# A two-layer hybrid encoder step: the eight PSUM banks of the first layer shared out anew

## The chip, the cores and the metric

The kernel runs on one core of a Trainium2 chip. A core has five engines, each with its own queue of instructions that it takes strictly in order: TensorE (PE in the profile; its weight loads are listed apart as PEld), VectorE (DVE), ScalarE (ACT), GpSimd (POOL) and SyncE (SP), which here mainly issues DMAs. TensorE writes its results into PSUM, 128 partitions wide, which this kernel uses as eight banks of 512 float32 columns. The other engines read PSUM and work on SBUF. Engines wait for each other through semaphores.

The metric is the device time of one execution in microseconds (us), lower is better.

## The reference

The kernel computes one inference step of two layers. Only the first layer's token mixer matters here: chunk-band attention with 16 heads of 64 channels, 2048 prompt rows, a band of 512 earlier rows, a learned bias by relative distance, and a gate path z from the same projection.

```python
def a_project(h, w_in, g_q, g_k):
    q, k, v, z = jnp.split(h @ w_in, 4, axis=-1)
    q = rms_norm(q.reshape(B, L, A_HEADS, A_HEAD_DIM), g_q)
    k = rms_norm(k.reshape(B, L, A_HEADS, A_HEAD_DIM), g_k)
    ...
def one_chunk(args):                      # 64 query rows against 512 + 64 key rows
    ...
    return attend(qi, kb, vb, rel_bias(table, qpos, kpos),
                  chunk_mask(qpos, kpos, A_BAND_CHUNKS), scale)
def attend(q, k, v, bias, mask, scale):
    s = jnp.einsum('bqhd,bkhd->bhqk', q, k).astype(jnp.float32) * scale
    s = jnp.where(mask[None, None], s + bias[None], NEG_INF)
    p = jax.nn.softmax(s, axis=-1).astype(v.dtype)
    return jnp.einsum('bhqk,bkhd->bqhd', p, v)
...
y = (o * jax.nn.silu(z)) @ w_out
```

Before it, each layer computes shift, scale and gate from the conditioning vector (`silu(c) @ W_ada + b_ada`), and beside the prompt a second group of 32 "sample" rows goes through the same mixer with a cache. The second layer is latent attention and keeps its own sharing of PSUM.

## The kernel before

**Numbers as pairs.** Operands of the matmuls are split into a high and a low half, so one product is three matmuls (helper `mm3`, lines 189 to 191). A projection chain over 1024 channels is 24 matmuls (8 x 3) into one bank.

**Steps.** The first layer's prompt attention is a list of 32 steps: two halves of the sequence, in each of them 8 pairs of heads (`g`), and for each pair two blocks of 512 rows (`blk`). I call the two steps of one head pair a cycle. In a step stand side by side, written as Python generators whose pieces a plan places at fractions of the step:

- `scores` and `values` of this step, for two heads and up to eight key tiles each. `scores` takes a bank of the kind `st` (lines 629, 630), VectorE adds bias or masks (633 to 637), ScalarE takes the exponential twice (643 into P, 644 into Ph), VectorE makes the low half Pl (645), GpSimd sums (647). Two tiles later `values` adds Ph and Pl times v (656, 657) into the bank of the head's output, kind `av`, which is taken once per head.
- `evac`: when a head is done, ScalarE copies one half of that bank (666) and VectorE adds the other half (667, the bank's last reader).
- `finish` of the step before: ScalarE casts a sum (675), the head pair's sums go through TensorE (680, 681, kind `mx`), VectorE takes reciprocals (687) and multiplies the gate z (688) and the output ob by it (689).
- `project` for the next step: four chains of 24 matmuls of 128x384, each into a bank of the kind `mm`. ScalarE copies each chain's bank to SBUF (481) and squares it (484).
- `project_z` for the next step: one chain of 24 matmuls of 128x512, kind `mm`, copied by ScalarE (513) into one of two SBUF tiles named z. The copy for one step needs the tile that line 689 of an earlier `finish` has read.
- `prep` for the next step: transposes (561) and row maxima of the scores (591 to 608), kind `mx`. Its matmuls need QG, which a DMA on SP's queue brings (its issue is line 104, a helper).

In steps 21 to 31 pieces of the second layer's conditioning (`ada_piece`) stand among these, in the last two steps the sample rows' attention (`sample_a`).

**PSUM.** The eight banks are fixed tiles. `psum_pool` gives each kind a list of them, and `bank(tag)` hands them out in turn; a tag without a list of its own takes from the list `mx`. In the rows the banks of `mm` are bank_66 and bank_70, of `st` bank_74 and bank_78, of `mx` bank_82, bank_86 and bank_90, of `av` bank_94. Later stages call `psum_pool` anew with their own numbers.

**Order.** The code's order is a wish: a scheduler (the Tile framework) sets the final order of each engine's queue when the kernel is built, and it knows which bank a tile lies in. TensorE's queue is one line: a matmul that waits for its bank holds up everything behind it.

Of the kernel before, what the change touches and what calls it, by code (L numbers as in the profile page):

```python
# [99 lines left out]
def trunk(ctx: ExitStack, tc: tile.TileContext, I, O, stop=99):  # L100
# [14 lines left out]
    def psum_pool(**bufs):  # L115
        i = 0
        psum.clear()
        for tag, n in bufs.items():
            psum[tag] = list(range(i, i + n))
            i += n  # L120

    psum_pool(mm=2, st=2, mx=3, av=1)

    S.preload_act_table_set("natural_log_exp_and_others")

# [67 lines left out]
    def bank(tag):  # L193
        order = psum[tag if tag in psum else "mx"]
        order.append(order.pop(0))
        return banks[order[-1]]
# [66 lines left out]
        gnorm.append(gn)  # L263

    def ada_part(i, pair, row, gc, sc, gn, adab, modr):
        acc = [bank("mm") for _ in range(2)]
        for k in range(KT):
            w = row()
            dma(w, I["ada_w"][i, 128 * k:128 * k + 128, 1024 * pair:1024 * pair + 1024])
            for n in range(2):  # L270
                T.matmul(acc[n][0:2, :], cT[:, k, :], w[:, 512 * n:512 * n + 512],
                         start=(k == 0), stop=(k == KT - 1))
        for n in range(2):
            mr = modr[:, 512 * n:512 * n + 512]
            V.tensor_tensor(mr, acc[n][0:2, :], adab[:, 512 * n:512 * n + 512], ALU.add)
            ada_use(i, pair, n, mr)
# [17 lines left out]
    def ada_piece(i, pair, n, a, ws, mr):  # L294

        c0 = 1024 * pair + 512 * n
        if a == 0:
            dma(mr, bass.AP(I["ada_b"].tensor, I["ada_b"].offset + 3 * i * D + c0, [[0, 2], [1, 512]]))
        for k in range(4):
            dma(ws[k], I["ada_w"][i, 512 * a + 128 * k:512 * a + 128 * k + 128, c0:c0 + 512])  # L300
        yield
        acc = bank("mm")[0:2, :]
        for k in range(4):
            T.matmul(acc, cT[:, 4 * a + k, :], ws[k], start=(k == 0), stop=(k == 3))
        V.tensor_tensor(mr, acc, mr, ALU.add)
        if a == 1:
            ada_use(i, pair, n, mr)
# [217 lines left out]
            split_z(s["next_g"], 1)  # L525

    def sample_rows(w, n, sec, g):
        p = bank("mm")[:, 0:n]
        for k in range(KT):
            for a in range(2):  # L530
                T.matmul(p[0:64, :], hsT[:, k, :], w(k, a), start=(k == 0 and a == 0), stop=(k == KT - 1 and a == 1))
        zt = at1([128, 4, 128], "hs").rearrange("p j t -> p (j t)")[0:NS, 0:n]
        S.copy(zt, p[32:64, :])
        V.tensor_tensor(zt, p[0:32, :], zt, ALU.add)
        if sec == 3:
            dma(zs_d[3, :, 128 * g:128 * g + 128], zt)
            return
        for h in range(2):
            c0 = 128 * g + 64 * h
            dma(zs_d[0:3, :, c0:c0 + 64].rearrange("s t d -> t s d"),  # L540
                zt[:, 192 * h:192 * h + 192].rearrange("t (s d) -> t s d", s=3))
# [293 lines left out]
    def sample_a(sp):  # L835
# [55 lines left out]
        for quad in range(4):  # L891
# [8 lines left out]
            if quad < 3:  # L900
                load_k(quad + 1)
            yield
            s0, s1 = bank("mm"), bank("mm")
            for p, ks in ((s0, [(kp[:, 0, :], kp[:, 1, :]) for kp in kps]),
                          (s1[:, 0:32], [(kn[:, quad, p2, 0:32], kn[:, quad, p2, 32:64]) for p2 in range(2)])):
                for p2 in range(2):
# [13 lines left out]
            S.copy(vn[:, 0, :], VR[0:32, qc])  # L920
            V.tensor_tensor(vn[:, 1, :], VR[0:32, qc], f32(vn[:, 0, :]), ALU.subtract)
            yield
            o = bank("mm")
            vals = [(vh[:, t, :], twin(nc, vraw[quad])[:, t, :]) for t in range(4)]
            pv_blocks(o[:, 0:256], PT, vals + [(vn[:, 0, :], vn[:, 1, :])], 544)
            diag_out(o, r, VR[zr, :], quad)
# [799 lines left out]
    for i in range(len(items) + LAG + 20):  # L1726
# [12 lines left out]
        if i >= LAG and fifo:  # L1739
            u, t, p = fifo.pop(0)  # L1740
            values(u, t, p)
            if t == u["order"][-1]:
                evac(u)
                later.append((i + DEN, denom, u))
                if u["blk"] % 2 and u["hd"] % 2:
                    n, u0 = INV if u["hd"] < 15 else (7, 9, 10, 10, 11), units[u["i"] - 1]
# [3 lines left out]
        while later and later[0][0] <= i:  # L1750
            _, f, u = later.pop(0)
            f(u)
        if i >= 100 and i % 25 == 0 and wload:
            k, n = wload.pop(0)
# [144 lines left out]
    def row(name):  # L1899
        return et([NS, D], name)  # L1900
# [62 lines left out]
```

## Time and profile before

| | |
|---|---|
| three timed runs | 3886.15, 3889.08 (median), 3892.15 us |
| the profiled execution's own time | 3874.33 us |
| its span, first to last instruction | 3872.2 us |
| mean granted TensorE clock | 0.956 |
| PE busy | 3598.0 us (93%) |
| PE weight loads | 2831.9 us (73%) |
| DVE busy | 3023.3 us (78%) |
| ACT busy | 2016.7 us (52%) |
| POOL busy | 1622.4 us (42%) |

The first layer's attention lies between about 0 and 1640 us of the span; the change touches nothing after it. The page's chain of work that ended last runs to 61% through TensorE and to 20% through VectorE. In the rows below the granted clock (PEclk) is a share of full speed; 0.50 is the lower of two levels.

### The profile page before, as it was taken

What the parts mean: (1) busy time and instruction counts of PE and PEld (TensorE: products, weight loads), DVE (VectorE), ACT (ScalarE), POOL (GpSimd) and SP (SyncE); (2) the same over time, 40 slices, a digit from 0 to 9 for tenths busy, and PEclk for the clock granted to TensorE, in tenths of its full rate; (3) what the DMA queues carried; (4) which work ended last, traced back from release to release, by engine and by line L of the source; (5) the groups of instructions that cost most, each with busy time, mean ns of one, the idle gap of its engine ahead of it and who ended that gap; (6) DMA issues with size and microseconds to landing.
All of it is one profiled execution on the core that took longest, in us unless ns stands there. A gap on an engine that the chain in (4) does not pass through costs nothing.

```text
span 3872.2 us, 56118 instructions
## 1 busy us (share of the span) xinstructions
PE 3598.0 (93%) x17410; PEld 2831.9 (73%) x17410; DVE 3023.3 (78%) x6646; ACT 2016.7 (52%) x4854; POOL 1622.4 (42%) x1680
## 2 busy tenths in 40 slices
PE   7899999889999999899999999889999999998999
PEld 4788888767766777677878888666767667766887
DVE  4788988889988888876777766788888888784663
ACT  4444544655544444542234555566766667664542
POOL 0222223333333323441013444377777777774032
PEclk9899999989999999799999999889999999998999
DMA  5222222222233332354453666652323323223253
GB/s 175 64 58 60 72 77 59 78 80 67 63 104 96 94 92 78 117 182 130 131 173 126 194 192 193 177 153 69 84 70 83 87 73 84 61 76 102 88 175 126
DMA packets 445036, 412.96 MB, mean 107 GB/s; under 512 B 72392, under 2 KB 367356, under 8 KB 437696
## 3 DMA queue, kind: packets, MB, share of 16 engines
q1 hardware_dynamic: 444736, 409.37, 36.2%
q8 instruction: 138, 2.26, 0.3%
q14 instruction: 162, 1.33, 0.1%
HBM read 251.72 MB, written 140.10 MB: 101 GB/s over the span
## 4 chain that ended last, share of the span: by engine, by line
PE 61%; DVE 20%; ACT 6%; issue 5%; DMA 4%; POOL 3%; SPq 0%; ACTq 0%; DVEq 0%; POOLq 0%
PE bank L189 10%; PE bank L190 10%; PE bank L191 10%; PE bank L1512 3%; PE bank L1537 3%; PE bank L1539 3%; PE bank L1538 3%; PE bank L1573 2%; PE bank L1572 2%; DVE ez@69_1247 L687 2%; PE bank L1592 1%; PE bank L656 1%; PE bank L657 1%; PE bank L629 1%; PE bank L591 1%
## 5 line engine op out<-in xcount | busy, mean ns | idle before, releaser
L1513 DVE TENSOR_REDUCE mp@319_16907<-bank 128x1 f32<-128x512 f32 (+3 forms) x384 | 235.1, 616 | 63.7 <-PE bank L1512 61.4
L647 POOL TENSOR_TENSOR acc@61_858<-acc@61_858,P@63_885 128x256 f32<-128x256 f32 (+3 forms) x64 | 57.2, 894 | 212.7 <-ACT P@63_885 L643 110.8
L1513 DVE TENSOR_REDUCE mp@320_16908<-bank 128x1 f32<-128x512 f32 (+1 forms) x192 | 115.7, 619 | 20.2 <-PE bank L1512 16.2
L643 ACT ACTIVATE P@63_885<-bank 128x384 f32<-128x384 f32 (+3 forms) x128 | 52.7, 412 | 126.0 <-DVE bank L633 62.1
L647 POOL TENSOR_TENSOR acc@61_858<-acc@61_858,P@64_886 128x256 f32<-128x256 f32 (+3 forms) x64 | 57.4, 898 | 143.4 <-ACT P@64_886 L643 99.7
L687 DVE RECIPROCAL ez@69_1247<-ez@69_1247 128x128 f32<-128x128 f32 x128 | 116.0, 922 | 0.0
L647 POOL TENSOR_TENSOR acc@61_858<-acc@61_858,P@65_887 128x128 f32<-128x128 f32 (+3 forms) x64 | 57.2, 894 | 139.5 <-ACT P@65_887 L643 94.8
L643 ACT ACTIVATE P@65_887<-bank 128x128 f32<-128x128 f32 (+3 forms) x128 | 52.5, 410 | 111.4 <-DVE bank L637 59.1
L1546 ACT ACTIVATE P@432_22141<-bank 128x512 f32<-128x512 f32 (+2 forms) x156 | 83.6, 536 | 49.4 <-PE bank L1539 14.2
L1546 ACT ACTIVATE P@430_22139<-bank 128x512 f32<-128x512 f32 (+2 forms) x156 | 83.7, 537 | 49.0 <-PE bank L1539 15.1
L643 ACT ACTIVATE P@64_886<-bank 128x256 f32<-128x256 f32 (+3 forms) x128 | 52.3, 409 | 108.5 <-DVE bank L633 51.2
L647 POOL TENSOR_TENSOR acc@62_859<-acc@62_859,P@63_885 128x128 f32<-128x128 f32 (+3 forms) x64 | 58.5, 914 | 117.7 <-ACT P@63_885 L643 111.7
L1546 ACT ACTIVATE P@429_22138<-bank 128x512 f32<-128x512 f32 (+2 forms) x156 | 83.8, 537 | 43.5 <-PE bank L1539 17.4
L1546 ACT ACTIVATE P@431_22140<-bank 128x512 f32<-128x512 f32 (+2 forms) x156 | 83.5, 535 | 41.7 <-PE bank L1539 15.5
L647 POOL TENSOR_TENSOR acc@62_859<-acc@62_859,P@65_887 128x256 f32<-128x256 f32 (+3 forms) x64 | 55.1, 862 | 105.1 <-ACT P@65_887 L643 98.9
L647 POOL TENSOR_TENSOR acc@62_859<-acc@62_859,P@64_886 128x256 f32<-128x256 f32 (+3 forms) x64 | 54.7, 855 | 96.9 <-ACT P@64_886 L643 87.0
L149 POOL TENSOR_TENSOR ozl@169_14178<-ozl_@174_14186,ozh@167_14176 128x1024 fp32r<-128x1024 f32 x8 | 19.3, 2410 | 149.9 <-ACT ozh@167_14176 L148 149.7
L1563 DVE TENSOR_TENSOR bank<-bank,P@431_22140 128x512 f32<-128x512 f32 (+2 forms) x108 | 66.8, 619 | 11.6 <-ACT P@431_22140 L1546 9.8
L1563 DVE TENSOR_TENSOR bank<-bank,P@430_22139 128x512 f32<-128x512 f32 (+2 forms) x108 | 66.8, 618 | 11.4 <-ACT P@430_22139 L1546 10.3
L1563 DVE TENSOR_TENSOR bank<-bank,P@429_22138 128x512 f32<-128x512 f32 (+2 forms) x108 | 66.8, 618 | 10.6 <-ACT P@429_22138 L1546 9.0
L1563 DVE TENSOR_TENSOR bank<-bank,P@432_22141 128x512 f32<-128x512 f32 (+2 forms) x108 | 66.7, 618 | 9.1 <-ACT P@432_22141 L1546 8.2
L1547 ACT ACTIVATE Ph@421_22117<-bank 128x512 fp32r<-128x512 f32 (+1 forms) x128 | 72.8, 569 | 0.0
(2154 smaller groups left out, 14826.7 us busy)
## 6 DMA issues: line engine op xcount, KB each, us to landing
h<-hT@197_14210 SPq DMA_DIRECT2D x16, 1024.0 KB
N<-hl@383_17303 SPq DMA_DIRECT2D x32, 512.0 KB
N<-hl@384_17304 SPq DMA_DIRECT2D x32, 512.0 KB
wr@10_289<-in_a_w_in SPq DMA_DIRECT2D x64, 192.0 KB
wr@11_290<-in_a_w_in SPq DMA_DIRECT2D x64, 192.0 KB
xr@9_224<-in_ada_w SPq DMA_DIRECT2D x32, 256.0 KB
xr@8_223<-in_ada_w SPq DMA_DIRECT2D x32, 256.0 KB
h1@214_14229<-h SPq DMA_DIRECT2D x8, 1024.0 KB
```

The source lines that it names most:

```text
L189: T.matmul(out, lhs[0], rhs[0], start=start, stop=False)
L190: T.matmul(out, lhs[0], rhs[1], start=False, stop=False)
L191: T.matmul(out, lhs[1], rhs[0], start=False, stop=stop)
L643: S.activation(P[:, 0:w], st[:, 0:w], AF.Exp)
L647: G.tensor_tensor(u["acc"][:, qs], u["acc"][:, qs], P[:, 0:w], ALU.add)
L687: V.reciprocal(ez[:, cs], ez[:, cs])
L1512: T.matmul(X[:, 0:w], qz[0:n, js], kz[0:n, 512 * c:512 * c + w], start=True, stop=True)
L1513: V.tensor_reduce(mp[:, j, c:c + 1] if blk else m4[:, j:j + 1], X[:, 0:w], AX.X, ALU.max)
L1537: T.matmul(st[:, 0:w], kz[0:96, ks], ql[:, qs], start=True, stop=False)
L1538: T.matmul(st[:, 0:w], kz[0:n, ks], qz[0:n, qs], start=False, stop=False)
L1546: S.activation(P[:, 0:w], st[:, 0:w], AF.Exp)
L1563: V.tensor_tensor((u["acc"] if last else u["sum"])[:, qs], old, P[:, 0:w], ALU.add)
```

## The change

The first layer's list becomes one bank for projections (`mm`), two for scores, three for the maxima, two for the heads' outputs (`av`). The conditioning's sums (`ada_part`, `ada_piece`) and the sample rows (`sample_rows`, `sample_a`) no longer take from `mm`; their new tag `ad` has no list, so they take from `mx` in turn with the maxima, the transposes and the sums of `finish`. No instruction is added or removed; which bank each one names, what it waits for and the engines' order change. In the rows of after the bank of `mm` is bank_66, of `st` bank_70 and bank_74, of `mx` bank_78, bank_82 and bank_86, of `av` bank_90 and bank_94.

```diff
-    psum_pool(mm=2, st=2, mx=3, av=1)
+    psum_pool(mm=1, st=2, mx=3, av=2)
...
     def ada_part(i, pair, row, gc, sc, gn, adab, modr):
-        acc = [bank("mm") for _ in range(2)]
+        acc = [bank("ad") for _ in range(2)]
...
-        acc = bank("mm")[0:2, :]
+        acc = bank("ad")[0:2, :]
...
     def sample_rows(w, n, sec, g):
-        p = bank("mm")[:, 0:n]
+        p = bank("ad")[:, 0:n]
...
-            s0, s1 = bank("mm"), bank("mm")
+            s0, s1 = bank("ad"), bank("ad")
...
-            o = bank("mm")
+            o = bank("ad")
```

**The order of TensorE's queue.** Three places, each as the program of before has it and as the changed one has it. HT0 and wq are the operands of `project`, HT1 and wz those of `project_z`, Ph, Pl and VT those of `values`, QA, QG, KA and KG those of `scores` and `prep`.

Half 0, TensorE, from the score tiles behind a z chain to the first matmuls of the next projection, before:

```order
L629 MATMUL bank_78<-QA@45_606,KA10@26_559 128x128 [waits DVE_49,Activation_49]
L630 MATMUL bank_78<-QG@47_608,KG10@30_563 128x128
L189 MATMUL bank_66<-wq@12_293,HT0@0_117 128x384
L190 MATMUL bank_66<-wq@12_293,HT0@0_117 128x384
```

The same place after the change:

```order
L656 MATMUL bank_94<-Ph@56_853,VT10@34_567 128x512 [waits Pool_49]
L657 MATMUL bank_94<-Pl@59_856,VT10@34_567 128x512
L629 MATMUL bank_74<-QA@45_606,KA10@26_559 128x128 [waits DVE_49,Activation_49]
L630 MATMUL bank_74<-QG@47_608,KG10@30_563 128x128
L656 MATMUL bank_94<-Ph@57_854,VT10@34_567 128x384
L657 MATMUL bank_94<-Pl@60_857,VT10@34_567 128x384 [waits DVE_49]
L189 MATMUL bank_66<-wq@12_293,HT0@0_117 128x384 [waits Activation_49]
L190 MATMUL bank_66<-wq@12_293,HT0@0_117 128x384
L191 MATMUL bank_66<-wq@12_293,HT0@0_117 128x384
L189 MATMUL bank_66<-wq@13_294,HT0@0_117 128x384
L591 MATMUL bank_78<-KG00@28_561,QG@46_607 128x384 [waits DMAHW4_49]
```

The projection's first matmul has gained a wait for ScalarE (the copy of the z chain's bank), two pairs of `values` matmuls stand ahead of it, and four of its matmuls instead of nineteen stand ahead of the first maximum (line 591).

Half 0, TensorE, the end of the projection's first chain and the start of its second, before:

```order
L189 MATMUL bank_66<-wq@19_300,HT0@0_117 128x384
L190 MATMUL bank_66<-wq@19_300,HT0@0_117 128x384 [waits DVE_49]
L191 MATMUL bank_66<-wq@19_300,HT0@0_117 128x384
L189 MATMUL bank_70<-wq@12_293,HT0@0_117 128x384 [waits Activation_49]
L190 MATMUL bank_70<-wq@12_293,HT0@0_117 128x384
```

The same place after the change:

```order
L189 MATMUL bank_66<-wq@19_300,HT0@0_117 128x384
L190 MATMUL bank_66<-wq@19_300,HT0@0_117 128x384
L191 MATMUL bank_66<-wq@19_300,HT0@0_117 128x384
L189 MATMUL bank_66<-wq@12_293,HT0@0_117 128x384 [waits Activation_49]
L190 MATMUL bank_66<-wq@12_293,HT0@0_117 128x384
```

Both chains now lie in one bank, and nothing stands between the last matmul of the one and the first of the other.

Half 1, TensorE, the first `values` matmuls of a block's second head, before:

```order
L191 MATMUL bank_66<-HT1@4_119,wz@43_600 128x512
L656 MATMUL bank_94<-Ph@56_853,VT11@35_568 128x512 [waits DMAHW1_49,DVE_49]
L657 MATMUL bank_94<-Pl@59_856,VT11@35_568 128x512
L629 MATMUL bank_78<-QA@45_606,KA10@26_559 128x384
L630 MATMUL bank_78<-QG@47_608,KG10@30_563 128x384
```

The same place after the change:

```order
L191 MATMUL bank_66<-HT1@4_119,wz@43_600 128x512
L656 MATMUL bank_94<-Ph@56_853,VT11@35_568 128x512 [waits DMAHW1_49]
L657 MATMUL bank_94<-Pl@59_856,VT11@35_568 128x512 [waits DVE_49]
L629 MATMUL bank_74<-QA@45_606,KA10@26_559 128x384 [waits Activation_49]
L630 MATMUL bank_74<-QG@47_608,KG10@30_563 128x384
```

Line 656 has lost its wait for VectorE (line 667 of the head before); the order is the same.

## Rows read from the trace of the kernel before

**Rows 1.** Busy time by stretch: half 0, transition, half 1; columns named first.

```profile
core 0: us, PE busy (x) PEld busy (x) DVE busy (x) ACT busy (x) POOL busy (x), PEclk, DMA share, GB/s
130.00:700.00 570.00, 546.53 (x2893) 458.43 (x2892) 501.69 (x1232) 280.69 (x678) 167.85 (x180) 0.99 0.23 65
700.00:1035.00 335.00, 306.56 (x1497) 249.40 (x1496) 296.51 (x726) 183.38 (x470) 120.97 (x121) 0.94 0.26 74
1035.00:1530.00 495.00, 466.44 (x2189) 344.96 (x2187) 415.10 (x1002) 216.03 (x526) 164.06 (x171) 0.98 0.33 92
```

**Rows 2.** PE's waits in half 1: us in total, times, longest.

```profile
PE bank L656 <- DVE ob@66_1077 L667: 12.4, 5, 2.9
PE bank L656 <- DVE ob@67_1078 L667: 7.5, 5, 2.0
```

**Rows 3.** PE's waits in half 0, same columns.

```profile
PE bank L591 <- DMA QG@46_607<-QA@44_605: 9.6, 7, 1.5
PE bank L656 <- DVE ob@67_1078 L667: 3.2, 7, 0.7
```

**Rows 4.** PE's waits in the transition, 700 to 1035 us, same columns.

```profile
PE bank L189 <- ACT z@53_827 L513: 2.8, 1, 2.8
```

**Rows 5.** Timeline, half 1: start, length, engine, line, operation; brackets: idle before, releaser.

```profile
1245.98 0.49 SPq L104 DMA_DIRECT2D QG@46_607<-QA@44_605  x1
...
1247.11 0.67 DVE L667 TENSOR_TENSOR ob@66_1077<-bank,ob@66_1077 64x512 f32<-64x512 f32 x1
...
1247.84 0.79 PE L656 MATMUL bank<-Ph@56_853,VT11@35_568 128*128 128x512 f32 x1 [2.89 <-DVE ob@66_1077 L667]
...
1252.04 0.61 PE L591 MATMUL bank<-KG00@28_561,QG@46_607 64*128 64x384 f32 x2
```

**Rows 6.** Busy time and granted clock right behind the gaps of Rows 5, 7.

```profile
1247.90:1251.30 3.40, 3.40 (x9) 2.82 (x10) 3.28 (x7) 0.87 (x2) 1.18 (x1) 0.50 0.59 162
...
1300.80:1303.00 2.20, 2.20 (x10) 1.76 (x10) 2.12 (x4) 0.87 (x2) 1.02 (x1) 1.00 0.52 119
```

**Rows 7.** Timeline of half 1, the other head's gap.

```profile
1300.05 0.48 SPq L104 DMA_DIRECT2D QG@46_607<-QA@44_605  x1
...
1300.78 0.50 PE L656 MATMUL bank<-Ph@57_854,VT10@34_567 128*128 128x512 f32 x1 [1.67 <-DVE ob@67_1078 L667]
...
1303.20 0.62 PE L591 MATMUL bank<-KG01@29_562,QG@46_607 64*128 64x384 f32 x2
```

**Rows 8.** Timeline of half 0: ends of projection chains and their copies.

```profile
567.91 0.34 PE L191 MATMUL bank<-wq@19_300,HT0@0_117 128*128 128x384 f32 x1
...
568.28 0.48 ACT L481 COPY raw@22_435<-bank 128x384 f32<-128x384 f32 x1 [2.62 <-PE bank L191]
...
577.03 0.39 PE L191 MATMUL bank<-wq@19_300,HT0@0_117 128*128 128x384 f32 x1
...
578.51 0.47 ACT L481 COPY raw@22_435<-bank 128x384 f32<-128x384 f32 x1
```

**Rows 9.** Timeline of half 0: a z chain's end and the next projection.

```profile
559.77 0.39 PE L191 MATMUL bank<-HT1@4_119,wz@43_600 128*128 128x512 f32 x1
...
561.42 0.39 PE L189 MATMUL bank<-wq@12_293,HT0@0_117 128*128 128x384 f32 x1
...
563.70 0.58 SPq L104 DMA_DIRECT2D QG@46_607<-QA@44_605  x1
...
564.35 0.69 DVE L689 TENSOR_TENSOR ob@67_1078<-ob@67_1078,z@54_828 128x512 f32<-128x512 f32 x1
...
565.07 0.58 ACT L513 COPY z@54_828<-bank 128x512 f32<-128x512 f32 x1 [1.69 <-DVE ob@67_1078 L689]
...
566.44 0.73 PE L591 MATMUL bank<-KG00@28_561,QG@46_607 64*128 64x384 f32 x3 [1.51 <-DMA QG@46_607<-QA@44_605]
```

**Rows 10.** ACT's waits in the whole first layer, columns as in Rows 2.

```profile
ACT z@54_828 L513 <- DVE ob@67_1078 L689: 14.2, 8, 3.2
```

**Rows 11.** Busy time in half 0 behind that projection's start.

```profile
566.40:587.00 20.60, 20.55 (x101) 16.11 (x102) 17.55 (x50) 9.36 (x21) 4.76 (x5) 1.00 0.40 118
```

## The prediction

> **What bounds the kernel now.** I read the busy time by stretch first. In half 0 of the first layer TensorE works 546.5 of 570 us at full clock; VectorE follows with 501.7, ScalarE has half its time free [rows 1]. So half 0 is bound by TensorE's queue, with 4% of air: a matmul that is held up there holds up everything behind it, and little later air gives the time back. Behind 566.4 us the queue is busy for 20.55 of 20.60 us [rows 11]; what is pushed into that stretch goes straight into the end of the head pair. In half 1 there is 6% of air (466.4 of 495), in the transition 8% (306.6 of 335) [rows 1]. Next I read what ends TensorE's idle times. In half 1 it is the bank of the heads' outputs: line 656, the first values matmul of a head, waits for line 667, the previous head's last reader, 12.4 and 7.5 us in ten waits, the longest 2.9 [rows 2]. In half 0 the same wait is 3.2 us in seven, and the larger one is the DMA of QG ahead of line 591, 9.6 us in seven, one a head pair [rows 3]. So the second output bank attacks some 23 us, 20 of them in half 1, and the price is the second projection bank, most of it in half 0.
>
> **The wait that goes.** With two banks line 656 does not wait for line 667. The long gaps of half 1 (12.4 in five with a longest of 2.9 means four of some 2.9 and a rest) end at 1247.84 in the one shown [rows 5]. Behind it the clock falls to 0.50, its lower level of 1.2 GHz: nine matmuls take 3.40 us there, where ten take 2.20 at full clock [rows 6]. That is 0.38 against 0.22 each, 9 x 0.16 = 1.4 us more. So a gap costs 2.9 + 1.4 = 4.3. What is late next is QG: its DMA is issued at 1245.98, and in half 0 the same DMA released line 591 at 566.44 after an issue at 563.70, 2.7 us later [rows 5, 9]. So line 591 can't run before 1248.7; it runs at 1252.04 now. The gain is 3.3 of the 4.3, for four gaps 13. For the other head the gap is 1.67 us [rows 7], but QG, issued at 1300.05, arrives at about 1302.8, and line 591 stands at 1303.20 now: 0.4 left. Five of these give 2, the fifth of the first kind 1. Half 1 thus gives back 16, half 0 its 3.2, and the transition some 2, for which I take half 1's mean wait of 2 once: **-21**. The most it can be is all the waits and all of the slow clock, 12.4 + 7.5 + 3.2 + 4 x 1.4 = 29 and the 2: -31. The least, if QG arrives later by a us in each: -14.
>
> **The hand-off in one bank.** A projection chain's first matmul must now wait until ScalarE has copied the chain before it. The last matmul of a chain starts at 567.91, its copy ends at 568.28 + 0.48 = 568.76, 0.85 later [rows 8]; a released matmul starts 0.06 behind its releaser (line 667 ends at 1247.78, line 656 starts at 1247.84 [rows 5]). From the mean of 20.6 us for 101 matmuls [rows 11] one matmul is 0.2. With nothing between the two chains TensorE stands still for 0.85 + 0.06 - 0.2 = 0.7 us; each matmul of other work between them covers 0.2, four cover it all. That holds if ScalarE is free: at 577.03 the copy started 1.5 us after the chain's last matmul because other ScalarE work was ahead, and ended 1.95 after it [rows 8], which uncovered is 1.8. In the changed order the scheduler has filled most hand-offs. Per head pair of half 0 there are eight hand-offs between projection chains, z chains and sample rows' copies that matter: I count one with nothing between (the second order shown), one with one matmul, three with three to six, the rest with seven or more. That is 0.7 + 0.6 + 0.5 + 0.3 + 0.4 = 2.5, and 0.3 for a copy queued as at 577.03.
>
> **The z copy.** This is the term that decides. In half 0 the z chain's last matmul starts at 559.77, but its copy starts at 565.07, since line 689 of the finish before still reads the SBUF tile until 565.04 [rows 9]; ScalarE waits so eight times, 14.2 us [rows 10]. Today that is free: the next projection's first matmul is in the other bank and starts at 561.42. The 19th starts at 566.44 - 1.51 - 0.34 = 564.59, before line 591 waits for QG, so the pitch is 3.17 / 18 = 0.176 [rows 8, 9]. In the changed order the first of them waits for the copy, which ends at 565.65. Only four values matmuls have been put ahead of it (first order shown), and only four projection matmuls stand between it and line 591. From 565.7 to 566.4 four fit; the other fifteen, 15 x 0.176 = 2.6 us, move behind line 591, where the queue is full [rows 11]. The four values matmuls came from there, 4 x 0.2 = 0.8. Net +1.8 a head pair. The idle span ahead of the copy grows to about 3 us, and after 2.9 us the clock fell [rows 5, 6]; one such fall is 1.4. The clock's row with 1.67 us idle ahead shows no fall [rows 6, 7]. I take no fall in the middle value and all six in the bound.
>
> **The sum.** Half 0: six head pairs (the first of the seven is in the start) x (1.8 + 2.5 + 0.3) = +28; bounds 6 x 2.5 = 15 if line 689 comes a little earlier, and 6 x 7 = 42 with a fall of the clock and one more queued copy. Half 1: every hand-off has five or more matmuls between, which covers a copy that starts at once; one queued copy (1.0 uncovered) and a part of a z copy, 1.4 x 5 = +7; bounds 2 and 14. Transition: z copies lag there too, and one such wait already exists, 2.8 us at line 189 behind line 513 [rows 4]; air is there, so I take two of it for most, +5; bounds 0 and 15. Start: the first projections run one behind the other with nothing between, three hand-offs of 0.7 and a z chain that no longer overlaps, +4; bounds 2 and 6. The conditioning's and sample rows' chains in the banks of the maxima: nothing, since three banks turn there, and their waits are of the air in rows 1; at worst one 0.7 in each of eleven steps, which I leave to the bounds of half 1. Added 28 + 7 + 5 + 4 = 44, removed 21: **+23**. Against the profiled execution's own 3874.33 us that is 3897; the median of the three runs is 3889.08, 14.8 above it, and so the forecast is 3889 + 23 = 3912. With the bounds taken as independent, the likeliest case's own range is +5 to +42, 3894 to 3931.
>
> **The rivals.** *Faster.* The gaps of half 1 come back whole, -31, and line 689 moves ahead in VectorE's queue together with the values it serves, so that the z copy costs nothing and the queued copies are few: half 0 +9, half 1 +3, the rest +6, sum -13, 3876. For it speaks that the scheduler spread the hand-offs; against it that line 591 waits for QG today, whatever the banks. It decides from a z copy that costs under 1 us a head pair. *They cancel.* The same with the gain as I have it: -21 against 21, 3889. *Slower yet, by the clock.* If the two kinds of stops in half 0 (z copy and the hand-off with nothing between, soon after the QG wait) lower the clock twice in each head pair, 2 x 1.4 x 6 = +17 comes on top, 3929. The gap of 1.67 us with its clock of 1.00 speaks against it, the one of 2.89 for it [rows 6, 7]. The Trainium skill has this as a rule of its own: "TensorE: Matmul & The Clock Gate", section "A second HAM failure mode: psum-queue depth-cycling", tells of a kernel that cycles through PSUM banks and pauses shortly between groups of matmuls, whose clock swings between its two levels and loses throughput between bursts. By that rule the change would be slower for the clock alone; the trace agrees for its long gaps and disagrees for its short ones. *It does not do what it says.* The order excludes it: line 656 has lost its wait, and line 189 has gained one.
>
> **How the numbers follow.** A measurement of this kernel can tell about 0.2% from no change, that is 3881 to 3897. The forecast has 0.48, the clock's rival 0.12, the cancelling one 0.22, the faster one 0.18. The forecast's lower end touches the 3897 line, but so does the cancelling case's upper end. So faster 0.18, same 0.22, slower 0.60. The range reaches from the faster rival's upper half, 3878, to beyond the clock's rival, 3938.
>
> **What would show it.** TensorE's wait of line 656 for line 667 is gone from both halves. New waits appear: line 189 for ScalarE's line 513, about 3 us once a head pair in half 0, and line 189 for line 481, below 1 us each. The clock shows 0.50 nowhere in half 1 behind a values matmul; if it shows it in half 0 behind the z copy, the clock's rival has its part. A head pair of half 0, 570 / 7 = 81 us today [rows 1, 3], is some 4 us longer, one of half 1 some 2 shorter, and the first layer's end moves by the sum. I am wrong if line 513 no longer waits for line 689 in the changed kernel, or if TensorE finds as much air behind the wait as it lost ahead of it.

## The result and the profile after

The changed kernel takes 3994.03 us (median of four runs, 3980.01 to 4001.24) against 3890.61 us of before (3886.15 to 3901.47): ratio 1.0257, 95% interval 1.0221 to 1.0293. The forecast was 3912, its range ended at 3938. The direction was right, the loss is 103 us and not 23. The profiled executions lie further apart than the medians (spans 3999.4 and 3872.2); the stages below are of these two, so they add up to 127 us and not to 103. The page's first line of after, to be held against the table of before: ScalarE, VectorE and GpSimd are as busy as they were, TensorE is busy 90 us longer with as many instructions.

```profile
PE 3688.2 (92%) x17410; PEld 2910.1 (73%) x17410; DVE 3038.9 (76%) x6646; ACT 2017.7 (50%) x4854; POOL 1614.4 (40%) x1680
```

All of it is in the first layer. I cut the trace at the first matmul of the projections for steps 2, 14, 22 and 30, and where the last stage of the layer writes its first result (line 1040), 1679.5 us before and 1806.7 after. From there to the end both take 2192.7 us. The columns are the stretch, its length, TensorE's busy time (matmuls), the granted clock, the DMA share and GB/s. Before:

```profile
0.00:139.70 139.70, 112.47 (x468) 0.89 0.42 134
139.70:645.00 505.30, 484.90 (x2564) 0.99 0.23 65
645.00:1039.80 394.80, 362.48 (x1788) 0.95 0.26 73
1039.80:1480.20 440.40, 415.42 (x1922) 0.97 0.34 95
...
1480.20:1679.50 199.30, 173.72 (x791) 0.85 0.38 112
```

After, the same stretches:

```profile
0.00:137.00 137.00, 109.63 (x467) 0.93 0.44 140
137.00:705.80 568.80, 517.23 (x2569) 0.92 0.21 58
705.80:1128.20 422.40, 383.69 (x1785) 0.89 0.24 67
1128.20:1583.50 455.30, 430.50 (x1887) 0.92 0.32 91
...
1583.50:1806.70 223.20, 194.64 (x823) 0.79 0.34 102
```

| stage | length | TensorE idle | TensorE busy |
|---|---|---|---|
| start | -2.7 | +0.1 | -2.8 |
| half 0 (steps 2 to 13) | +63.5 | +31.2 | +32.3 |
| transition (14 to 21) | +27.6 | +6.4 | +21.2 |
| half 1 (22 to 29) | +14.9 | -0.2 | +15.1 |
| last two steps and sample rows | +23.9 | +3.0 | +20.9 |

The cut at step 30 does not part the two queues at the same matmul: before has 1922 matmuls in its half 1, the changed kernel 1887, and the rest stands in the last stage. Before's half 1 up to about as many matmuls as the changed kernel and z_later (below, 1899) have in theirs:

```profile
1039.80:1468.40 428.60, 403.62 (x1889) 0.98 0.34 97
...
1039.80:1473.30 433.50, 408.52 (x1901) 0.98 0.34 96
```

Over as many matmuls half 1 thus lost some 27 us and not 14.9, again with no more idle time (25.0 against 24.8), and the last stage some 12 and not 23.9.

Half of the loss in half 0, and nearly all of it elsewhere, is time in which TensorE does the same matmuls longer: the granted clock in half 0 fell from 0.99 to 0.92, in half 1 from 0.97 to 0.92.

**Half 0, where the idle time comes from.** TensorE's waits there (us in total, times, longest; before they were QG and line 667 [rows 3]):

```profile
PE bank L189 <- ACT z@54_828 L513: 17.4, 7, 2.8
PE bank L594 <- DMA KG00@28_561<-KA00@24_557: 12.6, 6, 2.3
PE bank L189 <- ACT raw@23_436 L481: 5.7, 13, 0.8
...
PE bank L189 <- ACT raw@22_435 L481: 3.0, 8, 0.6
```

The first is the z copy of the prediction, the last two are the hand-offs. The second is new to me. The z stop in the timelines of VectorE, ScalarE and TensorE of after (start, length, engine, line, operation; in brackets idle time before and what ended it):

```profile
606.00 0.69 DVE L689 TENSOR_TENSOR ob@67_1078<-ob@67_1078,z@54_828 128x512 f32<-128x512 f32 x1
...
606.72 0.59 ACT L513 COPY z@54_828<-bank 128x512 f32<-128x512 f32 x1 [1.69 <-DVE ob@67_1078 L689]
...
604.10 0.44 PE L657 MATMUL bank<-Pl@60_857,VT10@34_567 128*128 128x384 f32 x1 [0.41 <-DVE Pl@60_857 L645]
607.36 0.44 PE L189 MATMUL bank<-wq@12_293,HT0@0_117 128*128 128x384 f32 x1 [2.82 <-ACT z@54_828 L513]
```

This is the chain of [rows 9], line 689, line 513, with line 189 now hung on its end. What followed, in busy time by stretch (start and end, length, the five engines' busy time; the figure behind the engines is the clock, 1.00, 0.55, 0.50, 0.51, 1.00):

```profile
604.60:607.30 2.70, 0.00 (x0) 0.00 (x0) 2.61 (x4) 1.01 (x2) 0.04 (x1) 1.00 0.49 143
607.40:612.00 4.60, 4.60 (x14) 3.83 (x15) 4.00 (x11) 0.00 (x0) 0.00 (x0) 0.55 0.82 259
612.00:618.00 6.00, 6.00 (x17) 4.12 (x17) 1.79 (x7) 1.18 (x3) 0.72 (x1) 0.50 0.07 20
618.00:625.00 7.00, 6.43 (x22) 4.98 (x21) 3.35 (x12) 2.14 (x6) 0.28 (x1) 0.51 0.30 75
625.00:630.00 5.00, 5.00 (x27) 4.12 (x26) 4.80 (x10) 1.59 (x4) 0.92 (x2) 1.00 0.53 150
```

After an idle span of 2.8 us TensorE worked at the lower level for some 17 us, almost without a pause; the span of [rows 6] had lasted 3.4. At half speed 17 us do the work of 8.5, so by this estimate the stop cost 2.8 and then at most 8.5. It is one of the two longest: in half 0 the trace's clock falls eleven times, once for 3.4 us, eight times for 6.8 and twice for 17, five times at a z stop, five times at the next stop, and once behind shorter ones.

**The second stop.** The maxima's line 594 needs KG, which a DMA fetches once ScalarE has cast KA (line 564). Before, line 666, line 562 and that cast stood one behind the other:

```profile
520.01 0.58 ACT L666 COPY ob@67_1078<-bank 64x512 f32<-64x512 f32 x1
520.62 0.69 ACT L562 ACTIVATE QA@44_605<-bank,gqk 64x512 fp32r<-64x512 f32 x1
521.33 0.58 ACT L564 CAST KA00@24_557<-bank 64x512 fp32r<-64x512 f32 x1
```

After, the scheduler has put a tile's two exponentials ahead of it, and they wait for VectorE (ScalarE's rows, then the DMA's issue and TensorE's wait):

```profile
556.36 0.59 ACT L666 COPY ob@67_1078<-bank 64x512 f32<-64x512 f32 x1
558.34 0.49 ACT L643 ACTIVATE P@64_886<-bank 128x384 f32<-128x384 f32 x1 [1.40 <-DVE bank L637]
558.73 0.48 ACT L644 ACTIVATE Ph@55_852<-bank 128x384 fp32r<-128x384 f32 x1
559.10 0.68 ACT L562 ACTIVATE QA@44_605<-bank,gqk 64x512 fp32r<-64x512 f32 x1
559.80 0.58 ACT L564 CAST KA00@24_557<-bank 64x512 fp32r<-64x512 f32 x1
...
560.41 0.53 SPq L104 DMA_DIRECT2D KG00@28_561<-KA00@24_557  x1
...
562.82 0.29 PE L594 MATMUL bank<-KG00@28_561,QG@46_607 64*128 64x128 f32 x1 [2.33 <-DMA KG00@28_561<-KA00@24_557]
```

From line 666 to line 564 it was 1.32 us, now it is 3.44. Behind this stop too the clock fell, for some 7 us (same columns as above):

```profile
560.40:562.80 2.40, 0.09 (x2) 0.01 (x1) 1.88 (x4) 0.95 (x2) 0.00 (x0) 1.00 0.48 109
562.80:570.40 7.60, 7.58 (x32) 6.52 (x33) 4.41 (x16) 2.42 (x9) 2.29 (x3) 0.55 0.01 3
570.40:574.00 3.60, 3.60 (x24) 3.45 (x22) 2.39 (x7) 0.46 (x3) 1.05 (x3) 1.00 0.10 23
```

**Half 1.** Line 656's wait for line 667 [rows 2] is gone from the list, as forecast. These stand in its place:

```profile
PE bank L591 <- DMA QG@46_607<-QA@44_605: 9.7, 9, 1.6
PE bank L591 <- DVE KA01@25_558 L567: 6.0, 4, 1.5
```

Where a gap of 2.89 us stood in the middle of the z chain [rows 5], two stand now behind its end, and the clock stays down for 10 us instead of 3.4 (TensorE's timeline, then the stretches):

```profile
1235.28 0.61 PE L591 MATMUL bank<-KG00@28_561,QG@46_607 64*128 64x384 f32 x2 [0.96 <-DMA QG@46_607<-QA@44_605]
...
1238.04 0.39 PE L591 MATMUL bank<-KG00@28_561,QG@46_607 64*128 64x256 f32 x1 [1.47 <-DVE KA01@25_558 L567]
```

```profile
1234.30:1239.40 5.10, 2.67 (x12) 1.79 (x11) 4.91 (x12) 2.21 (x6) 1.41 (x2) 0.99 0.63 171
1239.40:1249.60 10.20, 10.20 (x32) 7.94 (x31) 7.64 (x23) 2.72 (x10) 3.03 (x5) 0.50 0.13 39
1249.60:1253.00 3.40, 3.40 (x10) 0.60 (x9) 1.83 (x4) 0.62 (x1) 0.12 (x1) 1.00 0.47 129
```

### The profile page after: what moved, and what is told of

Same layout as the page of the kernel before. It is cut to its first block, busy times and chain, and to the rows that moved or that the text cites. A ratio compares the mean times of both kernels' runs of the same rounds, so it can differ in the third digit from the quotient of the medians.

```text
span 3999.4 us, 56147 instructions
## 1 busy us (share of the span) xinstructions
PE 3688.2 (92%) x17410; PEld 2910.1 (73%) x17410; DVE 3038.9 (76%) x6646; ACT 2017.7 (50%) x4854; POOL 1614.4 (40%) x1680
## 4 chain that ended last, share of the span: by engine, by line
PE 60%; DVE 21%; ACT 7%; issue 5%; DMA 3%; POOL 3%; SPq 0%; ACTq 0%; DVEq 0%; POOLq 0%
PE bank L189 10%; PE bank L190 10%; PE bank L191 10%; PE bank L1512 3%; PE bank L1537 3%; PE bank L1539 3%; PE bank L1538 3%; PE bank L1573 2%; PE bank L1572 2%; PE bank L1592 1%; DVE ez@69_1247 L687 1%; DVE Pl@60_857 L645 1%; PE bank L656 1%; PE bank L657 1%; PE bank L591 1%
## 5 line engine op out<-in xcount | busy, mean ns | idle before, releaser
L643 ACT ACTIVATE P@64_886<-bank 128x256 f32<-128x256 f32 (+3 forms) x128 | 52.4, 410 | 146.3 <-DVE bank L633 90.1
L485 DVE TENSOR_REDUCE s<-hs@20_327 128x4 f32<-128x256 f32 x128 | 52.0, 406 | 30.9 <-ACT hs@20_327 L484 30.3
L1563 DVE TENSOR_TENSOR bank<-bank,P@431_22140 128x512 f32<-128x512 f32 (+2 forms) x108 | 66.7, 618 | 11.4 <-ACT P@431_22140 L1546 9.6
L1563 DVE TENSOR_TENSOR bank<-bank,P@430_22139 128x512 f32<-128x512 f32 (+2 forms) x108 | 66.6, 617 | 11.1 <-ACT P@430_22139 L1546 10.0
L1563 DVE TENSOR_TENSOR bank<-bank,P@429_22138 128x512 f32<-128x512 f32 (+2 forms) x108 | 66.7, 618 | 10.0 <-ACT P@429_22138 L1546 8.4
L180 ACT ACTIVATE rt<-ms 128x12 f32<-128x12 f32 (+7 forms) x184 | 38.5, 210 | 69.6 <-DVE ms L174 42.0
```

What stands on the lines that cost most here:

```text
L643: S.activation(P[:, 0:w], st[:, 0:w], AF.Exp)
L1563: V.tensor_tensor((u["acc"] if last else u["sum"])[:, qs], old, P[:, 0:w], ALU.add)
```

## The experiments

Ratios are to the kernel before, measured on the same chip in the same rounds. The stages (us, with TensorE's idle time and the clock) are from the same cuts as above, each from one trace. Like stretches differ from trace to trace: half 0 with two projection banks and one output bank took 498.1 to 511.3 us, half 1 with one output bank and the z chain at its old place 433.7 to 440.4. A smaller difference than that is not shown by a single pair.

| run | ratio (95%) | start | half 0 | transition | half 1 |
|---|---|---|---|---|---|
| before | 1 | 139.7 | 505.3 (20.4; 0.99) | 394.8 | 440.4 (25.0; 0.97) |
| changed | 1.0257 (1.0221 to 1.0293) | 137.0 | 568.8 (51.6; 0.92) | 422.4 | 455.3 (24.8; 0.92) |
| ad_only | 0.9971 (0.9944 to 0.9998) | 134.9 | 511.3 (21.1; 0.97) | 399.1 | 438.0 (26.0; 0.97) |
| mm1_one_out | 1.0069 (1.0041 to 1.0096) | 132.4 | 553.8 (55.5; 0.93) | 396.4 | 433.7 (28.2; 0.98) |
| mm2_two_out | 1.0055 (1.0031 to 1.0079) | 143.8 | 500.3 (22.7; 1.00) | 405.0 | 447.5 (21.4; 0.93) |
| padded_z | 1.0162 (1.0114 to 1.0210) | 145.4 | 550.5 (29.5; 0.97) | 409.0 | 450.9 (22.2; 0.92) |
| mm1_alone | 1.0174 (1.0139 to 1.0209) | 137.8 | 557.4 (51.4; 0.93) | 412.0 | 436.4 (27.1; 0.98) |
| z_three | 1.0187 (1.0156 to 1.0219) | 146.3 | 529.2 (36.6; 0.98) | 418.5 | 449.9 (26.4; 0.94) |
| padded_both | 1.0232 (1.0201 to 1.0264) | 145.1 | 540.2 (29.3; 0.99) | 423.6 | 456.3 (23.4; 0.96) |
| two_out_padded | 1.0139 (1.0108 to 1.0170) | 145.2 | 507.8 (21.6; 0.97) | 426.4 | 468.1 (23.2; 0.94) |
| z_later | 1.0191 (1.0160 to 1.0222) | 138.0 | 572.0 (52.2; 0.91) | 430.5 | 426.5 (24.6; 1.00) |
| mix_one | 0.9975 (0.9956 to 0.9993) | 132.3 | 498.1 (18.5; 0.99) | 413.1 | 436.0 (26.6; 0.97) |
| mix_two | 0.9966 (0.9944 to 0.9989) | 132.7 | 505.4 (24.6; 0.98) | 401.8 | 438.3 (26.3; 0.96) |
| old_z_later | 0.9977 (0.9964 to 0.9989) | 137.2 | 507.5 (20.6; 0.98) | 400.3 | 431.0 (26.2; 0.99) |
| mix_late | 0.9959 (0.9941 to 0.9977) | 132.9 | 503.9 (18.8; 0.97) | 418.6 | 425.6 (23.2; 1.00) |

**Which part of the change.** Three kernels take the change apart by the shares of the banks; all edits stand against the changed kernel.

In the order ad_only, mm1_one_out, mm2_two_out:

```diff
-    psum_pool(mm=1, st=2, mx=3, av=2)
+    psum_pool(mm=2, st=2, mx=3, av=1)
...
+    psum_pool(mm=1, st=2, mx=4, av=1)
...
+    psum_pool(mm=2, st=2, mx=2, av=2)
```

> The changed kernel with the old shares (two projection banks, three for the maxima, one for the heads' outputs); only the conditioning's and the sample rows' sums stay in the banks of the maxima. Theory (one projection bank costs, sharing does not): within 0.2% of before, 3883 to 3898 us. Rival (the shared banks hold up maxima and sample rows): 20 to 40 us slower than before, with waits of the maxima's matmuls for the readers of sample sums.

3893.23 us against 3898.91: the shared banks cost nothing that can be seen; the ratio, 0.9971, even lies a little below 1.

> One projection bank, one bank for the heads' outputs, the eighth bank goes to the maxima (four). Theory (the loss is the single projection bank: the z copy's wait, a DMA wait that the new order opens, and the clock behind both): 100 to 130 us slower than before, 3990 to 4020, with line 656's wait for line 667 back in the rows. Rival (the second output bank and the order it brings make the loss): at most 50 us slower than before.

3927.03, 28 us slower: the theory's range is missed, the rival's (at most 50) is met, but not for the rival's reason, since half 0 lost 48 us of the changed kernel's 63 without the second output bank. The other stages lost next to nothing: start came out 7 us shorter than before, the transition 2 longer, half 1 at 433.7 us for 1887 matmuls, 5 longer over as many. The fourth bank for the maxima was not neutral, so I ran one projection bank without it.

```diff
-    psum_pool(mm=1, st=2, mx=3, av=2)
+    psum_pool(mm=1, st=2, mx=3, av=1)
```

> One projection bank, three for the maxima, one for the heads' outputs; the eighth bank lies idle. It stands one bank (heads' outputs) away from the changed kernel and one (maxima) away from the run with one projection bank and four for the maxima, which came 27 us above before. Theory A (the fourth bank for the maxima had hidden half of what one projection bank costs): 3940 to 3970 us, the second output bank then costs the rest. Theory B (the second output bank is what makes the changed kernel slow): 3915 to 3930, as with four for the maxima. Theory C (one projection bank is all): 3985 to 4000.

3957.06 against 3890.68: theory A. Between this kernel and before lies one projection bank (and the sharing, which costs nothing), and it is +66 us while the eighth bank lies idle. Between it and the changed kernel lies the second output bank alone: 11 us in half 0, 10 in the transition, 19 in half 1. Its half 0 has the idle time of the changed kernel already (51.4 us to 51.6), its half 1 before's clock (0.98 to 0.97). But the idle time of half 0 is made up otherwise: the z stop is longer here, 4.1 us, the wait for KG00 shorter.

```profile
PE bank L189 <- ACT z@54_828 L513: 24.9, 7, 4.1
...
PE bank L594 <- DMA KG00@28_561<-KA00@24_557: 5.6, 5, 1.1
```

So both stops come with the single projection bank; why the two sums come out equal is not shown.

> Two projection banks, two for the heads' outputs, two for the maxima. Theory: line 656's wait for line 667 is gone at no price in projections, and half 1 gives back 5 to 20 us; the maxima with two banks cost up to 15: 3870 to 3895. Rival (the second output bank's order loses): over 30 us slower than before. Rival (three banks for the maxima are needed): lines 591 to 608 wait for VectorE 2 us or more in each step, over 40 us slower.

3921.15, 22 us slower: the theory's range is missed, and so are both rivals'. Half 0 got 5 us shorter, which is within the spread. Half 1 got 7 us longer (over as many matmuls 19) with less idle time (21.4 against 25.0): the clock, 0.93 against 0.97. So the loss of half 1 by the clock does not need the single projection bank. This kernel has two banks for the maxima where before has three, and no run parts that from the second output bank; the pair mm1_alone and the changed kernel, with three banks for the maxima in both, has the second output bank alone, at +18.9 us.

**Is it the clock?** In padded_z the z chains of half 0 end in ten more matmuls of a zero tile, which add nothing to the sum and fill the stops with work.

```diff
+    zero = const.tile([128, 128], F32R, name="zero")
+    V.memset(f32(zero), 0.0)
...
+            pad = 10 if k == KT - 1 and s["half"] == 0 else 0
-            mm3(p, ..., k == 0, k == KT - 1)
+            mm3(p, ..., k == 0, k == KT - 1 and not pad)
+            for i in range(pad):
+                T.matmul(p, zero, hT[:, k, 0, :], start=False, stop=i == pad - 1)
```

> The changed kernel with ten more matmuls of a zero tile (128x512 each, result unchanged) at the end of every z chain of half 0, in the stretch where TensorE now stands still for the z copy and for the DMA of KG00. 16 x 10 x 0.23 = 37 us of added TensorE work. Theory (it is the clock that falls behind these stops which costs most): the spans of granted clock 0.50 behind them go, half 0 gets 5 to 9 us a head pair shorter, 3925 to 3965. Rival (the stops themselves cost, the clock follows anyway): the padding hides in the stops at best, 3985 to 4000, or adds up to 37, 4030.

3966.69, 27 us less than the changed kernel by the medians and 37 by the ratios, with more work in it; the theory's range ended 2 us lower. Half 0 got 18.3 us shorter, 3 a head pair with the padding in it, where 5 to 9 were expected, and the clock still falls in it, four times for 34 us in all.

```profile
145.40:695.90 550.50, 520.98 (x2677) 0.97 0.21 58
```

There are 108 more matmuls here than in the changed kernel's row, 108 x 0.23 = 25 us, and the busy time rose by 3.7: by this estimate the rest of the work took 21 us less, at a clock of 0.97 instead of 0.92. Had only the idle time been filled, the stretch would have stayed as long as it was.

**Is it the z copy?** z_three gives z a third SBUF tile, with the space of a tile that holds rows of x and later conditioning weights; part of the second layer's conditioning is then computed from overwritten weights, by the same instructions.

```diff
-        return at1([128, D], "xr", bufs=2)
+        return at1([128, D], "xr")
...
-                    s["z"] = at1([128, 512], "z", bufs=2)
+                    s["z"] = at1([128, 512], "z", bufs=3)
```

> The changed kernel with three SBUF tiles for z instead of two, so that line 513 need not wait for line 689; paid for with one tile instead of two for the rows of x and the conditioning's weights, which can only slow start, transition and half 1. Read in half 0, head pairs 2 to 7. Theory (the z copy's stop and the fall of the clock behind it): TensorE's wait at line 189 for line 513 falls from 2.5 to under 1 us, and a head pair gets 6 to 10 us shorter. Rival (the other stops keep the clock down all the same): 2.5 us shorter at most.

3967.62 in all. Line 189's wait for line 513 is gone but for 0.3 us, and half 0 took

```profile
146.30:675.50 529.20, 492.63 (x2568) 0.98 0.22 61
```

39.6 us less than the changed kernel, 6.6 a head pair: the theory's 6 to 10. Of these 15.0 are idle time and 24.6 busy time, so the stops carry more than their own length behind them in the clock. But the z stop is not all that went; KG's stop, 12.6 us in the changed kernel, was halved in the same run:

```profile
PE bank L594 <- DMA KG00@27_560<-KA00@23_556: 5.7, 6, 1.1
```

So 6.6 is the price of a z stop and half of a KG stop together, and no run shows the z stop's alone. mm1_alone has KG's stop at this length (5.6) and all its z stops; from its half 0 to this one it is 28.2 us, 4.7 a head pair, for z stops of 4.1 us, but with one output bank instead of two.

**Half 1.** Padding in both halves, and the padded half 1 of the kernel with two and two banks, are the same edit with another condition.

> The changed kernel with ten matmuls of a zero tile at the end of every z chain, in both halves (half 0 alone gave 3967 us). In half 1 the stops behind the z chain are line 591's waits for QG and for line 567, some 2.4 us together, and the clock then stays at 0.50 for 10 to 14 us. Theory (the clock is half 1's loss too, and the stops only its trigger): the padding fills these stops, half 1 gets 4 to 6 us a head pair shorter, 3930 to 3950 us in all. Rival (half 1's loss is of another kind): the padding adds up to 37 us, 3965 to 4005.

> Two projection banks, two for the maxima, two for the heads' outputs (22 us above before), with the ten zero matmuls at the end of the z chains of half 1 alone. Theory (that kernel's loss is the 17 us at clock 0.50 in each head pair of half 1, behind stops that follow the z chain): 3870 to 3895 us, below or at before. Rival (the padding is uncovered there): 3930 to 3960.

3980.32 and 3945.12: both theories' ranges are missed, both rivals' are met. In half 1 the clock rose (0.92 to 0.96, and 0.93 to 0.94), but the padding was not hidden: half 1 took 456.3 and 468.1. TensorE's idle time there stayed (23.4 us after 24.8, and 23.2 after 21.4). I take it that the waits behind the z chain move with the queue, so that padding ahead of them moves them too; no run shows that by itself. Then I moved the z chain itself.

```diff
-            place(plan, project_z(nx), 5, *(P_Z if si else (0.7, 0.95)))
+            place(plan, project_z(nx), 5, *(((0.62, 0.92) if nx["half"] else P_Z) if si else (0.7, 0.95)))
```

> The changed kernel with the z chains of half 1 placed later in their step (0.62 to 0.92 of it instead of 0.5 to 0.8), so that their long matmuls stand behind the first maxima. In half 1 TensorE's idle time is the same with one and with two banks for the heads' outputs, but behind the stops the clock stayed at 0.50 for 10 to 14 us instead of 3.4; in the kernel before a part of the z chain stood behind the stop, in the changed kernel the maxima's short matmuls. Theory (what stands behind the stop sets how long the clock stays down): spans of 3.4 to 7 us, half 1 8 to 15 us shorter than the changed kernel's 455. Rival (it is the two stops close together): spans of 10 us or more, half 1 450 us or more.

3968.72, and half 1:

```profile
1140.50:1567.00 426.50, 401.95 (x1899) 1.00 0.34 95
```

28.8 us shorter than the changed kernel's and, over about as many matmuls (433.5 above), 7 shorter than before's, with about the same idle time of 24.6 us and not one fall of the clock. Both sides of the expectation are missed: I had awaited short falls or long ones. The waits are spread out (TensorE's timeline in one step):

```profile
1340.10 0.66 PE L561 MATMUL bank<-ident,raw@23_436 128*128 128x128 f32 x4 [1.29 <-DVE raw@23_436 L490]
...
1342.99 0.50 PE L657 MATMUL bank<-Pl@59_856,VT11@35_568 128*128 128x512 f32 x1 [0.56 <-DVE Pl@59_856 L645]
...
1348.48 0.38 PE L591 MATMUL bank<-KG00@28_561,QG@46_607 64*128 64x256 f32 x1 [0.56 <-DVE KA01@25_558 L567]
```

So this run does not tell what stands behind a stop from how long stops are and how close they stand. It does show that the changed kernel's half 1 loses by its clock: the idle time is the same.

> The old shares (two projection banks, three for the maxima, one for the heads' outputs, sums of conditioning and sample rows with the maxima) with the later z chains in half 1 (0.62 to 0.92). Half 1 of the changed kernel fell to 426 us with them; before has 440. Theory (the second output bank and the later z chain work together: line 656's wait for line 667 stays without it): half 1 432 to 445 us, 3880 to 3900 in all. Rival (the place of the z chain alone makes the gain, the second bank nothing): half 1 420 to 430, 3865 to 3882.

```profile
1045.00:1476.00 431.00, 404.77 (x1901) 0.99 0.34 95
```

3883.28 against 3893.99, within the theory's range. Half 1's 431.0 lies a microsecond outside the theory's stretch and outside the rival's. With one output bank the later z chain gives 7 us (438.0 in ad_only). z_later, with the second output bank, is another 4.5 shorter, and mix_late below comes to the same (425.6), but both have one projection bank where this run has two, and 4.5 is within the spread of like stretches. So a gain of the second bank of its own is not shown; if this is it, it is under a third of the 16 that I forecast.

**A better kernel.** Shares that change between stages, through the lists of banks; this is mix_one, and in mix_two the lists from step 1 are `mx=[4, 5], av=[6, 7]`:

```diff
-    psum_pool(mm=1, st=2, mx=3, av=2)
+    psum_pool(mm=1, st=2, mx=4, av=1)
...
+        if si == 1:
+            psum.update(mm=[0, 3], mx=[4, 5, 6], av=[7])
+        if si == 14:
+            psum.update(mm=[0], mx=[3, 4, 5, 6], av=[7])
```

> The list of banks is changed between stages: one projection bank and four for the maxima in start, transition and half 1, two projection banks and three for the maxima from step 1 to step 13, one bank for the heads' outputs throughout. From the stages of the runs so far: start 125 (132 before), half 0 505, transition 396 (395), half 1 434 (440): 10 to 15 us under before. Theory (what one projection bank costs is paid in half 0, where z copy and projections stand close): 3873 to 3888. Rival (the gain of four banks for the maxima came from an order that the switch does not keep): 3888 to 3905.

> As the run before it, with two banks for the maxima and two for the heads' outputs from step 1 to step 13, where that split took 500 us against 505. Theory: 15 to 20 us under before, 3868 to 3883. Rival as before: 3888 to 3905.

3882.69 and 3884.01 against 3894.42: within the first range, just above the second; by the ratios 10 and 13 us under before. The transition gave part of it back (413.1 and 401.8). With the changed kernel's shares from step 18 and the later z chains from there (`si == 18`: `mm=[0], mx=[4, 5, 6], av=[3, 7]`; before it the shares of mix_one's half 0):

> One projection bank and four for the maxima at the start, two projection banks, three for the maxima and one for the heads' outputs in half 0 and the transition, the changed kernel's split (one, three, two) from step 18, with the later z chains from there. From the stages of the runs: start 125, half 0 498 to 505, transition 395 to 405, half 1 426: 20 to 28 us under before, 3862 to 3875. Rival (the transition loses what half 1 gains, as in the two mixed runs, 402 and 413): 3876 to 3890.

3875.64 against 3893.99, ratio 0.9959 (0.9941 to 0.9977): faster than both kernels, about 16 us by the ratio, and the smallest of all the ratios, though the time lies between the theory's range and the rival's. Its interval overlaps those of mix_one, mix_two, old_z_later and also of ad_only (0.9971), which has the old shares and only the conditioning's and the sample rows' sums moved. These four have that too, so no run shows that shares switched between stages or a later z chain gain anything beyond it.

The rival's point holds as well: its transition took 418.6 us against 394.8.

## Why the prediction was wrong

**The clock was left out of the middle value.** This is the step that failed: "I take no fall in the middle value and all six in the bound", at 1.4 us each from [rows 6]. Half 0 has two falls in a head pair, behind the z copy's stop and behind KG's, and nearly all last 6.8 or 17 us, not 3.4; at half speed that is at most 3.4 or 8.5 each. On top of the idle time came 32.3 us of busy time. The bound for half 0 was +42; it is +63.5.

The price of 1.4 was one row's, and the trace of before had others. [rows 5, 6] show one of its four gaps of 2.9 us in half 1; two of the four were followed by 3.4 us at the lower level, these two by none and by 17 us (TensorE's timeline, then busy time by stretch with the clock behind the engines):

```profile
1354.77 0.50 PE L656 MATMUL bank<-Ph@55_852,VT11@35_568 128*128 128x512 f32 x1 [2.89 <-DVE ob@66_1077 L667]
...
1460.07 0.80 PE L656 MATMUL bank<-Ph@57_854,VT11@35_568 128*128 128x512 f32 x1 [2.90 <-DVE ob@66_1077 L667]
...
1354.80:1358.00 3.20, 3.20 (x14) 2.28 (x14) 3.08 (x6) 1.46 (x3) 1.19 (x1) 1.00 0.61 164
...
1459.50:1476.50 17.00, 16.43 (x38) 9.59 (x39) 8.98 (x23) 4.91 (x13) 5.27 (x6) 0.50 0.16 45
```

**The idle time came out near by luck.** Half 0's 28 less the 3 that go is +25, and TensorE's idle time rose by 31.2, but of other parts: z stops 17.4 (forecast 1.8 x 6 = 11), KG's stop 12.6 (none), hand-offs 8.7 (17), less some 8 for the QG wait, which went (not forecast), and 3 for line 667; smaller waits make up the rest.

**The rival by the clock** had the right mechanism, two falls in each head pair, and a chance of 0.12; its price of 17 us is a term mis-sized by half (half 0's busy time rose 32.3), and it had no price for transition and half 1, where TensorE's busy time rose by 21 and 15 more. The Trainium skill's section "A second HAM failure mode: psum-queue depth-cycling" in "TensorE: Matmul & The Clock Gate" says that short pauses between groups of matmuls in a kernel that cycles PSUM banks make the clock swing and cost throughput between bursts. This case's traces agree: half 0 with two projection banks was granted 0.97 to 1.00, with one 0.91 to 0.93, and with one 0.97 to 0.99 when the pauses were filled with zeros, or the z stop was gone and KG's halved. I had counted the row of 1.67 us without a fall against it; that one row could not decide. In the changed kernel's half 0 all eleven stops of 2.3 to 2.8 us have a fall at them (that of the last z stop lies just behind the cut), in before's half 1 three of the four gaps of 2.9, and of five QG stops of 1.5 us in before's half 0 one was followed by 10 us at 0.50, four by none.

**KG's stop was not in the sum.** I had read TensorE's queue and not ScalarE's: the new order there delayed the cast of KA by 2.1 us. It is 12.6 us of waiting. That the hand-offs came out smaller (8.7 us in 21 waits where I had 2.8 a head pair, 17) and that QG's wait went hid it in the total.

**The z copy.** Mechanism, place and length were right (2.8 us once a head pair, "about 3" forecast). Its price of 1.8 a head pair was not: z_three, which took the z stop and half of KG's, gave 6.6, of which 15.0 / 6 = 2.5 are idle and 4.1 busy time. An idle part of 2.5 fits the 2.6 of the pushed matmuls; my 0.8 off for the values matmuls pulled ahead does not show.

**The gain in half 1.** Line 656's wait went, and QG became what is late, as said. But the idle time went nowhere: 25.0 to 24.8. The step that failed is "3.3 of the 4.3": QG's arrival and the bank that line 567 still reads were taken as fixed, or not seen at all (line 567 has 6.0 us in four waits), and the slow clock as part of the gap that goes away with it. It stayed, three times as long in the step shown. -16 was forecast, +19 measured between mm1_alone and the changed kernel.

**Start and transition.** Start: +4 forecast, -2.7 measured, and 132.4 against 139.7 in mm1_one_out; a loss there is not shown. Transition: +3, measured +27.6, of which 21.2 is busy time. mm1_alone took 412.0 there, but mm1_one_out, also with one projection bank, 396.4, and z_later, with the changed kernel's shares, 430.5; how the 27.6 divide between the two banks is not shown.

**The sharing of the maxima's banks** cost nothing, as taken. The last two steps' +23.9 (some 12 over as many matmuls), at a lower clock (0.85 to 0.79), were in no term; I did not test them apart.

**What stays open.** How long the clock stays down behind a stop: 3.4 us in [rows 6], 7, 10 and 17 here, with TensorE busy nearly throughout. What stands behind the stop does not settle it alone: before's four gaps of 2.9 us all had the end of a z chain behind them and were followed by 3.4, 3.4, none and 17. z_later does not tell whether the spacing of the stops decides. And why the scheduler moved ScalarE's exponentials ahead of the casts when one projection bank was left: the order shows that it did, not why.

## What to carry to other kernels

Where TensorE is the bound, price a new stop with what its clock does afterwards and not with its length: here half 0's stops brought 31 us of idle time and 32 us of slower work. A bank taken from a chain that runs all the time cost more here than the wait it removed elsewhere, above all since the chain's reader itself waits for SBUF; and when an allocation feeds a scheduler, read the new order of every engine that feeds the stalled one, not only of the bounding one. A wait that is removed moves the next ones together; where they end up, and which long matmuls are left to stand among them, decided here between 455 and 426 us for the changed kernel's half 1. And a price read from one row is a guess where the same trace holds other rows of the same kind.

## What was not expected of the hardware

The lower clock level lasts very differently: 3.4 us behind a gap of 2.89 us [rows 5, 6], some 17 behind one of 2.82, some 7 behind one of 2.33, 10.2 behind 0.96 and 1.47 in one step, though TensorE was busy almost throughout in each. In one trace, that of before, four gaps of 2.9 us, each with the end of a z chain behind it, were followed by 3.4, 3.4, none and 17 us of it. Adding some 25 us (an estimate, 108 x 0.23) of useless matmuls to half 0 made it 18 us shorter (568.8 to 550.5).
